# A longer plan for the gated DeltaNet loop, its gates in two buffers, and a new order of transfers around the loop

## The chip, the cores and the metric

The kernel runs on one core of a Trainium2 chip. TensorE (PE) multiplies, VectorE (DVE), ScalarE (ACT) and GpSimd (POOL) do elementwise work, and SyncE (SP) issues the DMA transfers. The metric is the device time of one execution in microseconds, as the median of several runs.

## The reference

A two-layer encoder over one sequence of 1024 tokens, 1024 wide, in float32. Layer 0 mixes tokens by softmax attention, layer 1 by a bidirectional gated DeltaNet; both are followed by a gated MLP with a width-3 convolution.

```python
# attention, 8 heads of 128, 2 kv heads
q, k, v, gate = split(rmsnorm(h) @ w_in)
o = softmax(rope(norm(q)) @ rope(norm(k)).T) @ v * sigmoid(gate);  h += o @ w_out
# gated DeltaNet, 8 q/k heads, 16 v heads of 128, both directions summed
qkv, z, ab = split(rmsnorm(h) @ w_in)          # z: one gate row block for each v head
q, k, v = split(silu(depthwise_conv5(qkv)))
S = S * exp(g) + k.T @ (u - (w @ S));  o = q @ S + attn @ v_new     # chunk by chunk
h += (rmsnorm(o_fwd + o_bwd) * silu(z)) @ w_out
# MLP, 2816 wide, after each mixer
a, b = split(depthwise_conv3(rmsnorm(h) @ w_up));  h += (silu(a) * b) @ w_down
```

## The kernel before

The program has four stages in a row: attention (L230), MLP 0 (`ffn_layer`, L352), gated DeltaNet (`gdn`, L878), MLP 1, and a last norm. Each float32 matrix product is done as three products of a high and a low part (`dense`, L126): `split` (L108) casts a tile to its high part on ACT (L109) and subtracts it on DVE or POOL for the low part (L110), so each block of weights costs a DMA, an ACT cast and a subtraction before PE can use it.

**The DeltaNet loop.** The q, k, v and z products of eight heads, their 5-tap convolutions, the inverses of the chunks' triangular matrices, two chains of eight chunk steps for each head (one in each direction) and the heads' outputs are six flows that a planner, `Weave` (L983), merges into one order for PE. A flow yields pairs: the PE time it has just issued, and an allowance, the plan time that must go by before it is asked again. `mark(name, after)` sets a plan time from which a flow that yielded that name may go on. Flows are asked in the order chains, inverses, prepare, decays, heads_out, products, so the products (L450) fill what the others leave. Only PE's order comes from the plan (`manual_schedule`); the other engines' order comes from a scheduler that goes by priority, and `ahead(n)` (L79) raises the priority of what is issued inside it. Each engine then works through its list in order, whatever the plan's times were.

The places that the change touches: `products` loads and splits the weights, multiplies (PE L490 in `steps`), and either convolves the row (`conv5`: ACT L443, four DVE L446, ACT silu L447) and marks it 20 us later, or, for a z row, takes silu and writes it to DRAM. `prepare` (L494) transposes the rows (PE L576) for k, the grams (PE L547) and the v rows. `heads_out` (L842) squares a half head's output o, multiplies the sums on DVE (L859, twice), raises them to a power (DVE L152, POOL L153, DVE L861), scales o on POOL (L863, eight times), and after an allowance of 16 us transposes it (PE L871), multiplies by the gate tile z (DVE L872) and stores it to DRAM as `od`. z is loaded by DMA at L868 into one buffer; it is overwritten by L872 and stored from there (L873). PSUM holds two `mm` tiles for products, one bank `sp` for all transposes and grams, one bank `ip` for inverses and two `cp` for chains.

**Around the loop.** The first half of the output projection (heads 0 to 3) is the last part of the products flow; the second half (`out_proj`, L326) follows the loop and reads heads 4 to 7 back from `od` through `split_rows` (DMA L941), staged in two slots of `w_raw`. In attention, the first four score blocks (`Heads.first`, L1369; PE L1387, ACT exp L1393) stand together ahead of the eight gate projections (ACT sigmoid L291). The MLP's up-projection (L1021) uses seven half-size products for eight; `operands` forms sums of weight blocks (L1125), and for the first two f takes spare tiles of `gp`. The down-projection (L1187) does the same over 11 blocks p: product 11, 21 (into four `sp` banks), t1 (same banks again), t2, and so on; t1's weights are s = a21 + a22 (DVE L1270), residuals are loaded into `res` tiles.

Of the kernel before, what the change touches and what calls it, by code (L numbers as in the profile page):

```python
# [18 lines left out]
P = 128  # L19
# [22 lines left out]
class Trunk:  # L42
# [187 lines left out]
    def attention(self):  # L230
# [3 lines left out]
        with ExitStack() as ctx, ExitStack() as right:  # L234
# [9 lines left out]
            with tc.tile_pool(reuse_waits="tile", name="yp", bufs=KT) as yp, tc.tile_pool(reuse_waits="tile", name="rp", bufs=1) as rp:  # L244
# [73 lines left out]
                for h in range(1, NH):  # L318
                    gate(h, proj(NH + 2 + h))
            olo = ctx.enter_context(tc.tile_pool(reuse_waits="tile", name="olo", bufs=1))  # L320
            with tc.tile_pool(reuse_waits="tile", name="qp", bufs=2) as qp, tc.tile_pool(reuse_waits="tile", name="pt", bufs=4) as ptp:
# [30 lines left out]
    def ffn_layer(self, layer):  # L352
        tc = self.tc
        xd = self.spill_h(f"xf{layer}_", PARTS)
        with ExitStack() as ctx:
            down = DownProjection(self, layer, xd, ctx)
            with tc.tile_pool(reuse_waits="tile", name="us", bufs=1) as us:
                up = UpProjection(self, layer, us, down.gp)
# [91 lines left out]
    def products(self, ys, tmp, begun):  # L450


        nc, w, cw = self.nc, self.ap["gdn_in"], self.cw5
        rows = [(j, n, i) for j in range(8) for n, i in (("k", 8 + j), ("q", j), ("z0", 32 + 2 * j), ("v0", 16 + 2 * j),
                                                        ("v1", 17 + 2 * j), ("z1", 33 + 2 * j))]
        parts = [(i, k) for _, _, i in rows[2:] for k in (0, 4)]
        split = []

        def fetch():
            if len(split) < len(parts):  # L460
                i, k = parts[len(split)]
                with self.ahead(1):
                    split.append(self.weights(w[i][:, k:k + 4]))

        fetch()
        for p, (j, name, i) in enumerate(rows):
            if p < 2:
                acc = begun[p]
            else:
                acc = self.big()  # L470
                for h in range(2):
                    fetch()
                    for step in self.steps(acc, split[2 * p - 4 + h], ys[4 * h:4 * h + 4], HALVES, h == 0, h == 1):
                        yield step
            if name[0] == "z":
                self.gate_rows(2 * j + int(name[1]), acc, tmp)
            else:
                with self.ahead(2):
                    self.rows[j, name] = self.conv5(acc, cw[:, i], tmp)
                self.weave.mark((name, j), 20.0)  # L480
        for step in self.first_out():
            yield step
# [11 lines left out]
    def prepare(self, tmp, dp):  # L494
# [5 lines left out]
        for j in range(8):  # L500
# [16 lines left out]
            for h, hs in enumerate(HALVES):  # L517
                t = tmp.tile([P, H2], F32, name="h", bufs=2)
                nc.scalar.copy(out=t, in_=self.transposed(kT[:, hs]))
                sums(t, ss[0][:, 4 * h:4 * h + 4])  # L520
                kn.append(t)
                yield 0.44, 1.2
            r = self.rstd(ss[0], 1, dp)
            for h, hs in enumerate(HALVES):
# [4 lines left out]
                put(2, kn[h], slice(4 * h, 4 * h + 4))  # L529
            yield 0.0, 9.0  # L530
            for h, hs in enumerate(HALVES):
# [23 lines left out]
            for h, hs in enumerate(HALVES):  # L555
                sums(self.transposed(qT[:, hs]), ss[1][:, 4 * h:4 * h + 4])
                yield 0.44, 2.8
            r = self.rstd(ss[1], 1, dp)
            self.rq.append(dp.tile([P, NC, 2], F32, name="rq", bufs=2))
            nc.vector.tensor_scalar(out=self.rq[j], in0=r.unsqueeze(2).broadcast_to([P, NC, 2]),  # L560
                                    scalar1=float(P) ** -0.5, scalar2=None, op0=ALU.mult)
            for e in range(2):
                yield f"v{e}", j
                v = self.rows[j, f"v{e}"]
                for h, hs in enumerate(HALVES):
                    t = tmp.tile([P, H2], F32, name="h", bufs=2)
                    nc.scalar.copy(out=t, in_=self.transposed(v[:, hs]))
                    put(3 + e, t, slice(4 * h, 4 * h + 4))
                    yield 0.44, 1.2
            self.weave.mark(("rows", j), 5.0)  # L570
# [271 lines left out]
    def heads_out(self, dp):  # L842
# [3 lines left out]
        for j in range(8):  # L846
            od = [self.dram.tile([P, S], F32, name=f"od{2 * j + e}") for e in range(2)]
            for i in (1, 0):
# [13 lines left out]
                for m in range(8):  # L862
                    nc.gpsimd.tensor_scalar(out=of[:, m], in0=of[:, m], scalar1=rs[:, m:m + 1], scalar2=1.0,  # L863
                                            op0=ALU.mult, op1=ALU.mult)
                yield 0.0, 16.0
                for e in range(2):
                    z = dp.tile([P, H2], F32, name="z", bufs=1)
                    nc.sync.dma_start(out=z, in_=self.zd[2 * j + e][:, hs])  # L868
# [4 lines left out]
                    nc.sync.dma_start(out=od[e][:, hs], in_=z)  # L873
                    yield 0.44, 1.5
            self.od += od
            self.weave.mark(("head", j))

    def gdn(self):  # L878
        nc, tc, ap = self.nc, self.tc, self.ap
        self.pk, self.rq, self.zd, self.od = [], [], {}, []  # L880
        with ExitStack() as left, ExitStack() as right:
# [18 lines left out]
            tc.cur_priority += 1000000  # L900
            oy, st = [], []
            self.outs, self.rows, self.grams, self.decayed, self.solved = {}, {}, {}, {}, {}

            def first_out():
                yps.close()
                oy.append(left.enter_context(tc.tile_pool(reuse_waits="tile", name="oy", bufs=KT)))
                st.append(left.enter_context(tc.tile_pool(reuse_waits="tile", name="st", bufs=1)))
                yield "head", 3
                os = self.split_rows(self.od[:8], oy[0], [slice(0, S)], lambda: tmp.tile([P, S], F32, name="t"))
                yield 0.0, 6.0  # L910
                for m in range(KT):
# [4 lines left out]
                    for i, hs in enumerate(HALVES):  # L916
                        r = st[0].tile([P, H2], F32, name="r")
                        nc.sync.dma_start(out=r, in_=xd[m][:, hs])
# [102 lines left out]
class UpProjection:  # L1021

    def __init__(self, trunk, layer, us, gp):
        self.t, self.nc, self.us, self.gp, self.b = trunk, trunk.nc, us, gp, trunk.b
        self.w = trunk.ap["ffn_up"][layer]
# [100 lines left out]

    def product(self, acc, ops, name, onto=False):

        x, col = ops[name]
        hi, lo = self.t.pair(self.t.wp, "w", H2)
        self.t.split(x, hi, lo, self.nc.gpsimd if name in ("p6", "p4") else self.nc.vector)
        w = [(hi[:, k * P:(k + 1) * P], lo[:, k * P:(k + 1) * P]) for k in range(4)]
        self.t.dense(acc, w, self.b[col], [slice(0, H2)], onto=onto)

    def run(self, up, down):
# [8 lines left out]
        for f in range(NFF):  # L1146
# [13 lines left out]
            with t.ahead(early):  # L1160
# [26 lines left out]
class DownProjection:  # L1187
# [52 lines left out]
    def run(self):  # L1240
# [11 lines left out]

        def product(name, x, accs, ms=range(4), ys=None, onto=False):
# [9 lines left out]

        def residual(m, i):
            r = gm.tile([P, H2], F32, name="res", bufs=3)
            nc.sync.dma_start(out=r, in_=self.xd[m][:, HALVES[i]])
            return r

        def add(out, x, z, engine=nc.vector):
            engine.tensor_tensor(out=out, in0=x, in1=z, op=ALU.add)  # L1270

# [15 lines left out]
        b = [t.bank() for _ in range(4)]  # L1287
        for m, acc in product("11", w1, a, ys=lambda p: self.ready[p] if p < G_FIRST else self.tokens("11", p)):
            add(h(m, 0), acc, residual(m, 0))
# [13 lines left out]
        b = [t.bank() for _ in range(4)]  # L1303
        for m, acc in product("t1", w5, b):
            add(h(4 + m, 1), acc, residual(4 + m, 1))

        def w6(p):
# [3 lines left out]
            return weights(s[p])  # L1311

        for m, acc in product("t2", w6, a, onto=True):
            add(h(m, 1), acc, residual(m, 1))
        for m, acc in product("t3", lambda p: weights(sub(a21[p], a11[p], a21[p])), a, onto=True):
# [8 lines left out]
        for m, acc in product("t4", w4, a, onto=True):  # L1324
            add(h(4 + m, 0), acc, residual(4 + m, 0))
            done(4 + m, 0, False)
# [21 lines left out]
class Heads:  # L1348
# [187 lines left out]
```

## Time and profile before

| | |
|---|---|
| median of 3 runs | 3536.3 us (3531.94 to 3542.98) |
| profiled execution, its own time | 3547.57 us |
| its span | 3545.4 us |
| mean granted TensorE clock | 0.963 |
| PE busy | 3263.7 us (92%) |
| DVE busy | 2478.2 us (70%) |
| ACT busy | 1732.9 us (49%) |
| POOL busy | 922.7 us (26%) |

PE is busy for most of the span, so what matters is where PE stands idle and what it then waits for, and where its granted clock is at the lower of its two levels (1.2 instead of 2.4 GHz, shown as 0.5 of full speed). The loop with its planner runs from 1369.1 to 2734.6 us; attention and MLP 0 come before, the output projection's second half, MLP 1 and the last norm after.

### The profile page before, as it was taken

The numbers are of one execution on the slowest core, as the hardware profiler recorded it, in microseconds if no ns is written. First come the engines' busy times: TensorE is split into PE (matmuls) and PEld (weight loads), VectorE is DVE, ScalarE is ACT, GpSimd is POOL, SyncE is SP. The second block draws the span as 40 slices with busy tenths as digits, with TensorE's granted clock in tenths as the row PEclk, the third lists the DMA queues.
The fourth block names the chain that finished last, engine by engine and source line by source line (L and its number), as shares of the span: only waits on it lengthen the run. The fifth ranks groups of instructions, "written<-read, shape, count | busy, mean of one in ns | idle before, by whom it ended". The sixth has DMA issues, their size and how long they took to land. (4 is left out here: it accounts for less than half of the span.)

```text
span 3545.4 us, 54292 instructions
## 1 busy us (share of the span) xinstructions
PE 3263.7 (92%) x19690; PEld 2649.4 (75%) x19690; DVE 2478.2 (70%) x4199; ACT 1732.9 (49%) x3212; POOL 922.7 (26%) x1111
## 2 busy tenths in 40 slices
PE   7999999799999998897898978989889989999998
PEld 6877878677778786686776866767667867777776
DVE  5325886878776866686776767576754778777685
ACT  4225664445444444455554645556442545454443
POOL 1111220444441001123232313232212154444100
PEclk9999999999999999998999989999899989999999
DMA  3331107333325633233333323333245733322553
GB/s 123 104 108 56 37 28 220 99 110 101 107 87 191 192 121 99 79 103 102 101 116 97 109 88 100 98 99 116 85 153 170 245 107 97 113 95 98 196 164 110
DMA packets 249228, 410.17 MB, mean 116 GB/s; under 512 B 25472, under 2 KB 76032, under 8 KB 248960
## 3 DMA queue, kind: packets, MB, share of 16 engines
q1 hardware_dynamic: 248960, 406.71, 36.5%
q8 instruction: 155, 2.54, 0.3%
q14 instruction: 113, 0.93, 0.1%
HBM read 293.76 MB, written 107.61 MB: 113 GB/s over the span
## 5 line engine op out<-in xcount | busy, mean ns | idle before, releaser
L490 PE MATMUL mm<-base,wh 128*128 128x512 f32 x864 | 389.3, 451 | 15.3 <-DVE t L446 14.8
L110 DVE TENSOR_TENSOR wl<-w_raw,wh 128x512 fp32r<-128x512 f32 x271 | 191.6, 710 | 196.2 <-ACT wh L109 174.6
L109 ACT CAST wh<-w_raw 128x512 fp32r<-128x512 f32 x271 | 167.1, 618 | 305.2 <-PE mm L134 108.4
L153 POOL TENSOR_TENSOR rs<-rs,power 128x8 f32<-128x8 f32 (+2 forms) x38 | 68.0, 1788 | 867.3 <-DVE rs L152 864.8
L109 ACT CAST wh<-s 128x512 fp32r<-128x512 f32 x216 | 134.1, 621 | 230.9 <-PE sp L134 118.0
L109 ACT CAST wh<-a 128x512 fp32r<-128x512 f32 x164 | 101.7, 621 | 261.9 <-PE mm L134 129.7
L134 PE MATMUL sp<-base,wh 128*128 128x512 f32 (+1 forms) x672 | 212.6, 375 | 7.6 <-ACT wh L109 6.7
L797 POOL TENSOR_SCALAR kd<-c,yds 128x128 f32<-128x128 f32 x224 | 96.1, 442 | 473.3 <-PE cp L829 368.1
L490 PEld LDWEIGHTS mm<-base,wh 128*128 128x128 f32 x864 | 168.2, 195 | 40.4 <-issue 15.3
L490 PE MATMUL mm<-base,wl 128*128 128x512 f32 x432 | 193.8, 449 | 0.0
L490 PE MATMUL mm<-yh,wl 128*128 128x512 f32 x432 | 174.4, 404 | 0.0
L446 DVE SCALAR_TENSOR_TENSOR t<-mm,gdn_cw,t 128x1023 f32<-128x1023 f32 (+1 forms) x128 | 163.0, 1276 | 15.0 <-ACT t L443 14.4
L490 PE MATMUL mm<-yl,wh 128*128 128x512 f32 x432 | 173.4, 401 | 0.2
L490 PE MATMUL mm<-yh,wh 128*128 128x512 f32 x432 | 173.4, 401 | 0.0
L110 DVE TENSOR_TENSOR wl<-s,wh 128x512 fp32r<-128x512 f32 x174 | 145.5, 837 | 25.9 <-ACT wh L109 25.5
L134 PE MATMUL sp<-base,wl 128*128 128x512 f32 (+1 forms) x432 | 158.7, 367 | 0.9 <-DVE wl L110 0.9
L134 PEld LDWEIGHTS sp<-base,wh 128*128 128x128 f32 x672 | 128.1, 191 | 30.8 <-ACT wh L109 9.5
L1125 POOL TENSOR_TENSOR s<-a,a 128x512 f32<-128x512 f32 x80 | 105.9, 1323 | 158.8 <-DVE s L1125 99.9
L1203 POOL TENSOR_TENSOR t<-t,t 128x512 f32<-128x512 f32 x66 | 102.6, 1554 | 126.4 <-DVE t L1181 124.6
L1396 POOL TENSOR_SCALAR p<-p,m 128x1024 f32<-128x1024 f32 x60 | 68.3, 1138 | 233.9 <-DVE m L1395 171.3
L110 DVE TENSOR_TENSOR gl<-raw,gh 128x512 fp32r<-128x512 f32 x132 | 97.2, 737 | 31.9 <-ACT gh L109 31.6
L110 POOL TENSOR_TENSOR wl<-s,wh 128x512 fp32r<-128x512 f32 x42 | 75.2, 1790 | 168.3 <-ACT wh L109 168.3
(535 smaller groups left out, 10162.8 us busy)
## 6 DMA issues: line engine op xcount, KB each, us to landing
a<-in_ffn_up_dram SPq DMA_DIRECT2D x160, 256.0 KB, 3.0
c<-pk SPq DMA_DIRECT2D x128, 320.0 KB, 3.0
w_raw<-in_gdn_in_dram SPq DMA_DIRECT2D x100, 256.0 KB, 2.9
g_t<-t SPq DMA_DIRECT2D x88, 256.0 KB, 2.0
raw<-g_t SPq DMA_DIRECT2D x88, 256.0 KB, 2.7
g<-t SPq DMA_DIRECT2D x66, 256.0 KB, 2.1
raw<-g SPq DMA_DIRECT2D x66, 256.0 KB, 3.0
a<-in_ffn_down_dram SPq DMA_DIRECT2D x66, 256.0 KB, 4.4
```

What stands on the lines that cost most here:

```text
L109: self.nc.scalar.copy(out=hi, in_=src)
L110: (engine or self.nc.vector).tensor_tensor(out=lo, in0=src, in1=hi.bitcast(F32), op=ALU.subtract)
L134: self.nc.tensor.matmul(acc if one else acc[:, hs], lhsT=a, rhs=y[:, hs], start=(first and not onto and k + t == 0), stop=(last and k == n ...
L153: nc.gpsimd.tensor_tensor(out=r, in0=v, in1=self.power[:, :w], op=ALU.pow)
L446: nc.vector.scalar_tensor_tensor(out=o, in0=a, scalar=c[:, i:i + 1], in1=o, op0=ALU.mult, op1=ALU.add)
L490: self.nc.tensor.matmul(acc[:, hs] if len(halves) > 1 else acc, lhsT=a, rhs=y[:, hs], start=(first and k + t == 0), stop=(last and k == n ...
L797: nc.gpsimd.tensor_scalar(out=kd[:, e], in0=kn, scalar1=col(self.yds, e), scalar2=1.0, op0=ALU.mult, op1=ALU.mult)
L1125: e.tensor_tensor(out=s[i], in0=x, in1=z, op=op)
L1203: sub = lambda out, x, z: nc.gpsimd.tensor_tensor(out=out, in0=x, in1=z, op=ALU.subtract)
L1396: nc.gpsimd.tensor_scalar(out=p, in0=p, scalar1=m[:, 3:4], scalar2=1.0, op0=ALU.mult, op1=ALU.mult)
```

## The change

The planner's allowances grow: 20 to 24 us behind a convolution, 9 to 15 behind the k norms, 1.2 to 2.0 behind transposes, 16 to 26 and 1.5 to 2.5 in the heads' outputs. The products flow waits for four marks, so that a product of the next head doesn't start before the rows or grams that it would crowd are through. The gate tile z gets two buffers, and its weights' splits higher priority. `r` (the residual of the output projection's first half) moves from a pool of its own to `tmp`'s "h". The reading back of heads 4 to 7 moves into `tmp`'s three "t" slots, ahead of the closing of that pool. In attention, four score blocks move between the gate projections. In the MLP, the first f has two more spare tiles and product p7's split is issued early; in the down-projection product 21's weight pairs come from the weights' pool instead of the tiles of a21 and a22, t1's work from p = 3 on is issued behind the adds that empty product 21's banks, and residuals are loaded straight into the tiles of h.

```diff
@@ attention()
                 for h in range(1, NH):
                     gate(h, proj(NH + 2 + h))
+                    if h < 5:
+                        heads.scores(0, self.base(3 + h, F32))
@@ Heads.first()
         self.queries(0, [self.t.base(k)[:, :H2] for k in (2, 3)])
-        for i in range(4):
-            self.scores(0, self.t.base(4 + i, F32))
@@ ffn_layer(): UpProjection gets down.rp too
@@ products()
-                with self.ahead(1):
+                with self.ahead(3):
                     split.append(self.weights(w[i][:, k:k + 4]))
...
             if p < 2:
                 acc = begun[p]
             else:
+                back = {"k": "queries", "z0": "first rows", "v0": "rows", "z1": "gram"}.get(name)
+                if back and (j or name == "z1"):
+                    yield back, j - (name != "z1")
                 acc = self.big()
...
-                self.weave.mark((name, j), 20.0)
+                self.weave.mark((name, j), 24.0)
@@ prepare()
                 kn.append(t)
-                yield 0.44, 1.2
+                yield 0.44, 2.0
...
-            yield 0.0, 9.0
+            yield 0.0, 15.0
...
+            self.weave.mark(("queries", j))
             r = self.rstd(ss[1], 1, dp)
...
                     put(3 + e, t, slice(4 * h, 4 * h + 4))
-                    yield 0.44, 1.2
+                    yield 0.44, 2.0
+                if e == 0:
+                    self.weave.mark(("first rows", j))
@@ heads_out()
-                yield 0.0, 16.0
+                yield 0.0, 26.0
                 for e in range(2):
-                    z = dp.tile([P, H2], F32, name="z", bufs=1)
+                    z = dp.tile([P, H2], F32, name="z", bufs=2)
...
-                    yield 0.44, 1.5
+                    yield 0.44, 2.5
@@ gdn()
-                        r = st[0].tile([P, H2], F32, name="r")
+                        r = tmp.tile([P, H2], F32, name="h", bufs=2)
...
+            os = self.split_rows(self.od[8:], oy[0], HALVES, lambda: tmp.tile([P, S], F32, name="t")[:, :H2])
             right.close()
-            os = self.split_rows(self.od[8:], oy[0], HALVES, lambda: self.wp.tile([P, H2], F32, name="w_raw", bufs=2))
@@ UpProjection.operands(): spare tiles for the first two f
-            free = iter([self.gp.tile([P, H2], F32, name=n) for n in (3 - f) * ("gh", "gl")])
+            free = [self.gp.tile([P, H2], F32, name=n) for n in (3 - f) * ("gh", "gl")]
+            free = iter(free if f else free + [self.rp.tile([P, H2], F32, name="raw") for _ in range(2)])
@@ UpProjection.product() and run()
+        with self.t.ahead(early):
+            self.t.split(x, hi, lo, self.nc.gpsimd if name in ("p6", "p4") else self.nc.vector)
...
-            self.product(a, ops, "p7", onto=True)
+            self.product(a, ops, "p7", onto=True, early=early)
@@ DownProjection.run()
             for p in range(NP):
-                w = x(p)
-                y = ys(p) if ys else self.tokens(name, p)
+                with t.tc.issue_after(after.ins) if after and p > 2 else nullcontext():
+                    w = x(p)
+                    y = ys(p) if ys else self.tokens(name, p)
...
-            r = gm.tile([P, H2], F32, name="res", bufs=3)
-            nc.sync.dma_start(out=r, in_=self.xd[m][:, HALVES[i]])
-            return r
+        def residuals(ms, i):
+            for m in ms:
+                nc.sync.dma_start(out=h(m, i), in_=self.xd[m][:, HALVES[i]])
...
-        w2 = lambda p: weights(self.load(a12[p], 0, 1, p), [one(n, p, F32R) for n in ("a21", "a22")])
-        for m, acc in product("21", w2, b):
-            add(h(m, 0), acc, h(m, 0))
+        for m, acc in product("21", lambda p: weights(self.load(a12[p], 0, 1, p)), b):
+            read = add(h(m, 0), acc, h(m, 0))
...
-        for m, acc in product("t1", w5, b):
-            add(h(4 + m, 1), acc, residual(4 + m, 1))
+        residuals(range(4, 8), 1)
+        for m, acc in product("t1", w5, b, after=read):
+            add(h(4 + m, 1), acc, h(4 + m, 1))
...
```

**Order of DVE ahead of head 4's output (first half).** `o<-cp,o` is a chain step, `L446`/`L448` a convolution tap, `ss<-ss,rq` (L859, after: L868) the sums from which the output's norm starts; `pr`, `at`, `al` are decays, `wk`, `w_...`, `x` inverses. Before:

```order
L604 TENSOR_TENSOR pr<-pr,qks 128x512
L607 TENSOR_TENSOR al<-at,ah 128x512
L688 STREAM_TRANSPOSE wk<-tp 128x512
L808 SCALAR_TENSOR_TENSOR r_22316<-cp,negc,c 128x128 x2
L814 SCALAR_TENSOR_TENSOR o<-cp,egc,o 128x128 x2
L690 COPY w_11722<-wk 32x16x32 x4
L596 SCALAR_TENSOR_TENSOR pr<-pr,ebias,maskneg 128x128 x4
L446 SCALAR_TENSOR_TENSOR t<-mm,gdn_cw,t 128x1023
L603 TENSOR_TENSOR at<-pr,kks 128x512
L446 SCALAR_TENSOR_TENSOR t<-mm,gdn_cw,t 128x1022
L604 TENSOR_TENSOR pr<-pr,qks 128x512
L859 TENSOR_TENSOR ss<-ss,rq 128x8
```

After:

```order
L697 STREAM_TRANSPOSE wk<-tp 128x512
L704 TENSOR_TENSOR x<-ip,lvl 128x512
L699 COPY w_11706<-wk 32x16x32 x4
L612 TENSOR_TENSOR at<-pr,kks 128x512
L605 SCALAR_TENSOR_TENSOR pr<-pr,ebias,maskneg 128x128
L613 TENSOR_TENSOR pr<-pr,qks 128x512
L605 SCALAR_TENSOR_TENSOR pr<-pr,ebias,maskneg 128x128 x3
L110 TENSOR_TENSOR wl<-w_raw,wh 128x512
L448 SCALAR_TENSOR_TENSOR t<-mm,gdn_cw,t 128x1022 x2
L448 SCALAR_TENSOR_TENSOR t<-mm,gdn_cw,t 128x1023 x4
L448 SCALAR_TENSOR_TENSOR t<-mm,gdn_cw,t 128x1022 x2
L868 TENSOR_TENSOR ss<-ss,rq 128x8 x2
```

Eight taps of two convolutions, in two runs of both kinds, now stand together ahead of the sums, where two taps stood among other work.

**Order of DVE between product 21 and t1 in MLP 0's down-projection.** `s_...<-a_...,a_...` is t1's weight sum (it needs two weight loads), `h_...<-sp` empties a bank of product 21. Before:

```order
L1270 TENSOR_TENSOR s_10051<-a_5_10029,a_5_10040 128x512
L110 TENSOR_TENSOR gl<-raw,gh 128x512
L1270 TENSOR_TENSOR s_10052<-a_6_10030,a_6_10041 128x512
L110 TENSOR_TENSOR gl<-raw,gh 128x512
L1270 TENSOR_TENSOR s_10053<-a_7_10031,a_7_10042 128x512
L1273 TENSOR_TENSOR a_7_10031<-a_7_9651,a_7_10031 128x512
L1270 TENSOR_TENSOR h_9495<-sp,h_9495 128x512
L1270 TENSOR_TENSOR h_9496<-sp,h_9496 128x512
L1270 TENSOR_TENSOR h_9497<-sp,h_9497 128x512
L1270 TENSOR_TENSOR h_9498<-sp,h_9498 128x512
```

After:

```order
L110 TENSOR_TENSOR gl<-raw,gh 128x512
L110 TENSOR_TENSOR wl<-base_9752,wh 128x512
L110 TENSOR_TENSOR gl<-raw,gh 128x512
L110 TENSOR_TENSOR wl<-s_10042,wh 128x512
L110 TENSOR_TENSOR gl<-raw,gh 128x512
L110 TENSOR_TENSOR wl<-s_10043,wh 128x512
L1280 TENSOR_TENSOR h_9495<-sp,h_9495 128x512
L1280 TENSOR_TENSOR h_9496<-sp,h_9496 128x512
L1280 TENSOR_TENSOR h_9497<-sp,h_9497 128x512
L1280 TENSOR_TENSOR h_9498<-sp,h_9498 128x512
```

Before, the four adds stand behind eight of the eleven sums; after, behind three (the first three sums stand further up, at s_10042 to s_10044).

**Order of SP at the end of the loop.** `od` is a head's stored output that is read back, `w_raw<-in_gdn_out_dram` the weights of the output projection's second half. Before:

```order
L121 DMA w_raw<-in_gdn_out_dram 128x512 x2
L941 DMA w_raw<-od_26782 128x512
L918 DMA r<-xd_11476 128x512
L941 DMA w_raw<-od_26783 128x512
L121 DMA w_raw<-in_gdn_out_dram 128x512 x2
L941 DMA w_raw<-od_20773 128x512
L920 DMA x_11874<-r 128x512
L941 DMA w_raw<-od_20774 128x512
L121 DMA w_raw<-in_gdn_out_dram 128x512
L341 DMA res<-x_11867 128x512
```

After:

```order
L882 DMA od_27110<-z 128x512
L949 DMA t<-od_27109 128x512
L949 DMA t<-od_27110 128x512
L949 DMA t<-od_21251 128x512
L949 DMA t<-od_21252 128x512
L949 DMA t<-od_23040 128x512
L949 DMA t<-od_23041 128x512
L949 DMA t<-od_25143 128x512
L949 DMA t<-od_25144 128x512
L949 DMA t<-od_27109 128x512
L949 DMA t<-od_27110 128x512
L121 DMA w_raw<-in_gdn_out_dram 128x512 x5
```

The weights stood among the reads of `od`, two loads after two reads; they now stand behind the reads of all four heads. The first two reads shown need the stores of head 7 just ahead of them, the other eight are the second halves of all rows.

## Rows read from the trace of the kernel before

**Rows 1.** Busy time by stretch: the loop, and two stretches at head 6's output.

```profile
core 0: us, PE busy (x) PEld busy (x) DVE busy (x) ACT busy (x) POOL busy (x), PEclk, DMA share, GB/s
1369.10:2734.60 1365.50, 1206.92 (x10154) 976.15 (x10154) 946.10 (x2115) 713.77 (x1565) 334.06 (x685) 0.94 0.35 107
2532.00:2544.00 12.00, 0.67 (x4) 0.27 (x2) 9.41 (x24) 3.14 (x4) 2.25 (x3) 0.66 0.13 44
2544.00:2556.00 12.00, 9.38 (x94) 6.96 (x94) 4.88 (x15) 4.66 (x18) 2.22 (x7) 0.78 0.22 67
```

**Rows 2.** PE's waits: what it waited for, us in total, times, longest.

```profile
PE sp L871 <- POOL o L863: 49.9, 19, 11.9
PE sp L576 <- DVE z L872: 26.2, 11, 3.8
PE sp L576 <- ACT t L447: 20.5, 3, 7.8
PE sp L134 <- ACT wh L109: 18.6, 4, 7.7
PE sp L134 <- DVE h L1270: 16.5, 2, 10.5
...
PE mm L490 <- DVE t L446: 14.8, 2, 10.7
PE sp L871 <- DVE z L872: 8.0, 2, 6.1
...
PE mm L1387 <- ACT base L1393: 4.7, 1, 4.7
...
PE sp L547 <- DVE z L872: 2.9, 1, 2.9
...
PE mm L1387 <- DVE base L110: 1.6, 1, 1.6
```

**Rows 3.** Timeline at head 6's output: start, duration, engine, line, tile, count, idle before.

```profile
2530.78 0.42 DVE L839 TENSOR_TENSOR o<-cp,o 128x256 f32<-128x256 f32 x1
...
2531.91 0.59 PE L805 MATMUL cp<-st,c 128*128 128x256 f32 x2
...
2536.20 1.28 DVE L446 SCALAR_TENSOR_TENSOR t<-mm,gdn_cw,t 128x1023 f32<-128x1023 f32 x1
...
2539.78 0.16 DVE L859 TENSOR_TENSOR ss<-ss,rq 128x8 f32<-128x8 f32 x1
...
2541.38 1.65 POOL L153 TENSOR_TENSOR ro<-ro,power 128x8 f32<-128x8 f32 x1 [16.60 <-DVE ro L152]
...
2543.40 2.81 POOL L863 TENSOR_SCALAR o<-o,ro 128x128 f32<-128x128 f32 x8 [0.37 <-DVE ro L861]
...
2543.83 0.48 PE L871 MATMUL sp<-ident,o 128*128 128x128 f32 x1 [11.33 <-POOL o L863]
```

**Rows 4.** Timeline at head 0's output, where z's one buffer is stored and loaded.

```profile
1627.25 0.74 DVE L872 SCALAR_TENSOR_TENSOR z<-sp,gdn_gain,z 128x512 f32<-128x512 f32 x1
...
1630.04 0.33 SPq L868 DMA_DIRECT2D z<-zd  x1
...
1633.90 0.74 DVE L872 SCALAR_TENSOR_TENSOR z<-sp,gdn_gain,z 128x512 f32<-128x512 f32 x1
```

**Rows 5.** ACT's timeline at a transposition of k that came late.

```profile
1607.47 1.28 ACT L447 ACT_TABLE_LOAD   x1
1608.77 1.06 ACT L447 ACTIVATE t<-t 128x1024 f32<-128x1024 f32 x1
```

**Rows 6.** Timeline of SP's queue and PE at the end of the loop.

```profile
2736.40 0.33 SPq L941 DMA_DIRECT2D w_raw<-od  x1
...
2738.23 0.32 SPq L941 DMA_DIRECT2D w_raw<-od  x1
...
2739.20 1.22 PE L134 MATMUL sp<-base,wh 128*128 128x512 f32 x2 [4.65 <-ACT wh L109]
...
2760.50 0.80 PE L134 MATMUL sp<-base,wh 128*128 128x512 f32 x2 [2.09 <-ACT wh L109]
```

**Rows 7.** ACT's timeline at the first scores, and two gate projections later on.

```profile
209.27 1.28 ACT L1393 ACT_TABLE_LOAD   x1 [6.55 <-DVE m L1391]
210.56 1.21 ACT L1393 ACTIVATE base<-mm,m,scale 128x1024 f32<-128x1024 f32 x1
...
240.35 1.02 ACT L291 ACTIVATE t<-mm 128x1024 f32<-128x1024 f32 x1
...
251.23 1.02 ACT L291 ACTIVATE t<-mm 128x1024 f32<-128x1024 f32 x1
```

**Rows 8.** DVE's timeline between product 21 and t1.

```profile
1159.25 0.69 DVE L1270 TENSOR_TENSOR s<-a,a 128x512 f32<-128x512 f32 x1 [1.70 <-DMA a<-in_ffn_down_dram]
...
1160.58 2.48 DVE L1270 TENSOR_TENSOR h<-sp,h 128x512 f32<-128x512 f32 x4
```

More of the change, by code (lines that the diff above doesn't have):

```diff
@@ L1 @@
-from contextlib import ExitStack, contextmanager
+from contextlib import ExitStack, contextmanager, nullcontext
 from functools import partial
@@ L357, in ffn_layer @@
             with tc.tile_pool(reuse_waits="tile", name="us", bufs=1) as us:
-                up = UpProjection(self, layer, us, down.gp)
+                up = UpProjection(self, layer, us, down.gp, down.rp)
                 up.tokens(self.gain_ffn[:, layer])
@@ L900, in gdn @@
             tc.cur_priority += 1000000
-            oy, st = [], []
+            oy = []
             self.outs, self.rows, self.grams, self.decayed, self.solved = {}, {}, {}, {}, {}
@@ L906, in first_out @@
                 oy.append(left.enter_context(tc.tile_pool(reuse_waits="tile", name="oy", bufs=KT)))
-                st.append(left.enter_context(tc.tile_pool(reuse_waits="tile", name="st", bufs=1)))
                 yield "head", 3
@@ L1021, with __init__ @@
 class UpProjection:
-    def __init__(self, trunk, layer, us, gp):
-        self.t, self.nc, self.us, self.gp, self.b = trunk, trunk.nc, us, gp, trunk.b
+    def __init__(self, trunk, layer, us, gp, rp):
+        self.t, self.nc, self.us, self.gp, self.rp, self.b = trunk, trunk.nc, us, gp, rp, trunk.b
         self.w = trunk.ap["ffn_up"][layer]
@@ L1127, in operands, with product @@
                 "p4": (a22, "t4"), "p3": (s[3], "22")}
-    def product(self, acc, ops, name, onto=False):
+    def product(self, acc, ops, name, onto=False, early=0):
         x, col = ops[name]
         hi, lo = self.t.pair(self.t.wp, "w", H2)
-        self.t.split(x, hi, lo, self.nc.gpsimd if name in ("p6", "p4") else self.nc.vector)
+        with self.t.ahead(early):
+            self.t.split(x, hi, lo, self.nc.gpsimd if name in ("p6", "p4") else self.nc.vector)
         w = [(hi[:, k * P:(k + 1) * P], lo[:, k * P:(k + 1) * P]) for k in range(4)]
@@ L1251, in weights, with product @@
             return pair
-        def product(name, x, accs, ms=range(4), ys=None, onto=False):
+        def product(name, x, accs, ms=range(4), ys=None, onto=False, after=None):
             for p in range(NP):
-                w = x(p)
-                y = ys(p) if ys else self.tokens(name, p)
+                with t.tc.issue_after(after.ins) if after and p > 2 else nullcontext():
+                    w = x(p)
+                    y = ys(p) if ys else self.tokens(name, p)
                 for m in ms:
@@ L1262, in product @@
             return [(m, accs[m]) for m in ms]
-        def residual(m, i):
-            r = gm.tile([P, H2], F32, name="res", bufs=3)
-            nc.sync.dma_start(out=r, in_=self.xd[m][:, HALVES[i]])
-            return r
+        def residuals(ms, i):
+            for m in ms:
+                nc.sync.dma_start(out=h(m, i), in_=self.xd[m][:, HALVES[i]])
         def add(out, x, z, engine=nc.vector):
-            engine.tensor_tensor(out=out, in0=x, in1=z, op=ALU.add)
+            return engine.tensor_tensor(out=out, in0=x, in1=z, op=ALU.add)
         def sub(out, x, z, engine=nc.vector):
@@ L1287, in run @@
         b = [t.bank() for _ in range(4)]
-        for m, acc in product("11", w1, a, ys=lambda p: self.ready[p] if p < G_FIRST else self.tokens("11", p)):
-            add(h(m, 0), acc, residual(m, 0))
+        acc11 = product("11", w1, a, ys=lambda p: self.ready[p] if p < G_FIRST else self.tokens("11", p))
+        residuals(range(4), 0)
+        for m, acc in acc11:
+            add(h(m, 0), acc, h(m, 0))
         a12 = [x[:, hs] for x in [t.base(i, F32) for i in range(2, 8)] for hs in HALVES][:NP]
-        w2 = lambda p: weights(self.load(a12[p], 0, 1, p), [one(n, p, F32R) for n in ("a21", "a22")])
-        for m, acc in product("21", w2, b):
-            add(h(m, 0), acc, h(m, 0))
+        for m, acc in product("21", lambda p: weights(self.load(a12[p], 0, 1, p)), b):
+            read = add(h(m, 0), acc, h(m, 0))
             done(m, 0, m == 0)
@@ L1311, in w6 @@
             return weights(s[p])
+        residuals(range(4), 1)
         for m, acc in product("t2", w6, a, onto=True):
-            add(h(m, 1), acc, residual(m, 1))
+            add(h(m, 1), acc, h(m, 1))
+        residuals(range(4, 8), 0)
         for m, acc in product("t3", lambda p: weights(sub(a21[p], a11[p], a21[p])), a, onto=True):
@@ L1324, in run @@
         for m, acc in product("t4", w4, a, onto=True):
-            add(h(4 + m, 0), acc, residual(4 + m, 0))
+            add(h(4 + m, 0), acc, h(4 + m, 0))
             done(4 + m, 0, False)
```

## The prediction

> **What bounds the kernel now.** I read the busy shares first (PE 92% of the span, DVE 70%), then PE's waits, then the timeline around the longest ones, and last the granted clock by stretch. PE is the bound: what can be won is its idle time, and the time that it works at the lower clock.
>
> In the loop PE is busy 1206.92 of 1365.50 us [rows 1], so 158.6 us are idle. The waits [rows 2] name three groups there. A: PE's transposition of a head's output waits for POOL's scaling, 49.9 us, of which four waits of 11 to 12 us are 46.5 and the rest crumbs. B: a transposition or gram waits for DVE's multiplication by z, 26.2 + 8.0 + 2.9 = 37.1. C: the transposition of k waits for the convolution's silu, 20.5 in three. Together 104.1. A further 14.8 is a product that waits at the start for convolutions to empty a PSUM tile.
>
> How A comes about [rows 3]: PE issues its last possible chain work at 2531.91 and then stands before L871. DVE took up the chain's step at 2530.78, at PE's pace, but has 9.0 us of other work in its list before the sums at 2539.78: taps of 1.28 us, decays, inverse copies. From there sums, power (1.65 on POOL) and first scaling take 4.05 us to L871 at 2543.83. Hence a rule: wait = W + 4.05 - Q, with W the DVE work between a chain step and the sums in DVE's list, and Q the PE work between the same step and L871 in PE's list. With the profile's durations the old lists give 11 to 12 for heads 3 to 6, and four waits of that size are there. The plan's allowance (16 us) doesn't see W.
>
> B [rows 4]: the one z tile is read by L872 at 1627.25, stored, loaded again from 1630.04, and used at 1633.90: 6.65 us in which the sp bank stays full. C [rows 5]: four taps wait in DVE's list, a table load of 1.28 us comes, silu takes 1.06.
>
> The clock in the loop is 0.94 of full speed [rows 1]: 0.06 x 1365.5 = 82 us of full-speed time is missing. Part of it falls into the waits themselves: at head 6 the 12 us with the wait ran at 0.66 (4.1 lost, mostly idle), the next 12 at 0.78 (2.6 lost, working). By that ratio 32 us would be lost to work, and 82 is the upper end.
>
> **The loop, term by term.** B: with two z tiles, both loads go out ahead of the head's output, and the sp bank is emptied 0.75 us after its transposition: -37. C: the mark moves from 20 to 24 us and the transpositions' allowances from 1.2 to 2.0; I take it all, -20.5. A: the allowance of 26 gives Q some 4 to 10 us more, but DVE's list changes too. In the order ahead of head 4, W is one stream transpose, one x, four copies, at, pr, wl (each about 0.6 net), four decays (1.1) and eight taps at 1.19 (9.5): 14.8, and Q counted from PE's order is 5.7: 14.8 + 4.05 - 5.7 = 13.2. Head 2 is alike (W 15.9, Q 5.8: 14.2), head 3 gives 5.4 + 4.05 - 7.1 = 2.4, heads 5 and 6 about nothing (W 8.1 and 10.1 against Q 11.9 and 12.2), but there the last product of a head waits for the tap that empties its PSUM tile, by the same count 6.6 and 6.5. Sum 43, with crumbs of 3 as now 46. So A, B and C together go from 104 to 46: **-58**. From the other side: if a plan with more room removed them all, -104; if the new lists gave nothing back, 0.
>
> Clock: the waits fall by 56%, so by the two ends above 18 to 46 us come back; the new waits are long ones, at whose end the clock is down, so I take **-20**. Start: the product z1 of head 0 now stands behind the first grams, so the wait of 10.7 [rows 2] shrinks, but six steps on the single sp bank have no product beside them, about 1.1 each (a transposition and its 0.6 copy): **-4**. A fuller loop meets DVE (946 us busy, 69% of it, 73% of a loop of 1290) more often; the idle time outside the named waits is 158.6 - 104.1 - 14.8 = 40, and I add an eighth, **+5**.
>
> End of the loop. Now the first L134 waits 4.65 and another 2.09 [rows 6]; the reads of `od` alternate with weight loads through two slots, 1.83 us apart. After the change the head's last transpositions stand directly before L134, where products stood between; the weights are queued on SP behind all reads, and the eight second-half reads go through three slots. Store about 2 (od at 1628.01 to the next load at 1630.04, the pair around [rows 4]), eight reads at 1.4 to 1.75 (two slots give about 2.6 a read over the stretch, three two thirds of it), then load 2.9 and cast 0.6: 2 + 13 + 3.5, about 20 instead of 6.7: **+13**. If the queue runs ahead, 0; if stores and reads don't overlap at all, +28. Loop and end: -64.
>
> **The other stages.** Attention: the waits 4.7 and 1.6 [rows 2] come from the scores standing together; spread between projections 10.9 us apart [rows 7], each block has a projection to hide reduction and exp. With 2.6 for the clock after it (the stretch after head 6's wait) that is -8.9. Exp and sigmoid alternate, six more table loads of 1.28 [rows 7]. An exp's load starts only when DVE is done (209.27, after 6.55 idle), but it lies under the next projection; a sigmoid's load carries no wait for PE and can go early, so I charge 1: **-8**. If the sigmoid's load lay on PE's path it would be 4 x 1.28 = 5.1 more, so -3; the chance of that is 0.2.
>
> The Trainium skill (ScalarE: Activation LUTs, "What ACT_TABLE_LOAD costs") speaks against the alternation: each change of set costs 2.66 us, 1283 ns of load and the rest a drain. The trace agrees on the load (1.28) and shows exp at 210.56 right after it, so no drain behind the load; were the full price on PE's path, the four would cost 10.6 and attention would be slower by 2.6.
>
> MLP up, both layers: the casts of p7 and t3 make 18.6 - 6.7 = 11.9 us of L134's waits. Two more spare tiles let the sums go without waiting for tiles, and the early split puts p7's cast ahead of later work; DVE remains busy there, so I take two thirds, -8, and 3 for the clock: **-11** (-2 to -16).
>
> MLP down, both layers: 16.5 [rows 2]. The four adds that empty product 21's banks took 2.48 us, but began only when eight sums had passed, each waiting for a weight load (1.70 before the last) [rows 8]. In the new order they stand behind three sums, whose loads no longer wait for product 21's pairs. What is left is the first add's 0.6 and a semaphore, 1.5 each: -13.5, and 2.6 of clock each: **-19**. What is late next is t1's own weights; there the residual loads, issued earlier on SP, could stand before them, at 0.4 us each: up to +3. Range -5 to -21.
>
> Sum: -64 - 8 - 11 - 19 = **-102**. The profiled execution took 3547.57, so 3445.6 for its like; it lies 11.3 above the median of the runs, and from the median 3536.3 the sum gives **3434 us**.
>
> **Rivals.**
> 1. DVE becomes the bound of the loop. For: its lists decide A and C, and allowances only move waits. Against: 946 us in 1365 leaves 420 idle. Then A stays at 46 with the taps' waits on top: 104 falls to about 90, clock gives 5, and the sum is -14 - 5 - 4 + 5 + 13 - 38 = -43: 3493.
> 2. The change doesn't do what it says at z: the second tile's load stands behind a store or a `pk` transfer on SP, so B stays (37 us, with 8 of clock): 3434 + 45 = 3479. For: SP is one list, and 37 us came through it. Against: the order has z's loads in pairs ahead of the transpositions.
> 3. Slower: the taps gather before the sums at every half head. Place: DVE's list between the chain step and L868. Eight taps instead of two to three add about 7 us to W; where Q doesn't grow, waits of 11.6 become 19, and over the seven heads 1 to 7 that is 133 instead of 104, clock +15. It decides once DVE's lag at a head passes the 26 us of allowance less 4. Sum: +29 + 15 + 13 - 38 + 5 = +24: 3560. For: heads 2 and 4 show it. Against: heads 3, 5, 6 don't.
>
> **How the numbers follow.** My forecast 0.60, alone with a range of 3395 to 3475 (from the loop's waits between 20 and 75 and its end between 0 and +28). Rival 1 0.20, rival 2 0.11, rival 3 0.09. To leave out no more than a fifth the range runs from 3395 to 3525. A measurement tells 0.3% (10.6 us) from no change, so faster means under 3525.7: all of my forecast and rival 2, most of rival 1: 0.86. Slower 0.08, none to be told 0.06.
>
> **What would show it.** In the new profile B's waits on z are gone, A's rows show two waits of 13 to 14 (heads 2 and 4) and none at 5 and 6, products waiting for taps appear with about 6 us, the first L134 after the loop waits near 20, the loop is near 1290 us. In the MLPs the wait on `h` falls to about 3 in total. Wrong: a loop above 1330 us, more than two waits over 10 us on POOL, or exp's table loads ending PE's waits.

## The result, and the profile after

The change made the kernel faster, by much less than forecast: 3517.78 us (median of 4) against 3538.47, ratio 0.9941 [0.9923, 0.9959], so -20.7 us where -102 were expected. The two profiled executions lie 33 us apart (spans 3545.4 and 3512.4), since that of before took longer than any of the four timed runs (3547.6 against at most 3543.0) and that of after is the fastest of its four; the sums by stage below go by these two, and so overstate the gain by 12 us in all.

| stretch | forecast | before | after | difference |
|---|---|---|---|---|
| up to the loop's first product | -23 | 1369.1 | 1354.3 | -14.8 |
| the loop | -77 | 1365.5 | 1348.8 | -16.7 |
| wait behind the loop | +13 | 4.65 | 20.14 | +15.5 |
| from there to the end | -15 | 806.2 | 789.2 | -17.0 |

Most of what is missing lies in the loop. Outside it these two executions look near the forecast, but the 12 us must be taken off somewhere, and x1 below measures less. Busy time of the loop after (columns as in [rows 1]):

```profile
1354.30:2703.10 1348.80, 1210.31 (x10154) 987.26 (x10154) 943.73 (x2116) 701.23 (x1556) 333.87 (x685) 0.94 0.37 109
```

The clock is 0.94 as before, the idle time 138 instead of 159. PE's waits in the loop after, which answer to [rows 2]:

```profile
PE mm L496 <- DVE t L448: 45.7, 5, 13.9
PE ip L669 <- DVE w L683: 18.1, 10, 11.2
PE sp L880 <- POOL o L872: 10.8, 16, 2.2
PE sp L880 <- DVE z L881: 9.5, 4, 4.5
PE sp L585 <- ACT t L449: 6.7, 2, 3.8
PE ip L764 <- ACT r L760: 6.3, 10, 2.0
PE sp L553 <- DVE kks L555: 5.7, 4, 3.3
PE cp L832 <- DVE r L817: 5.4, 5, 4.2
PE cp L813 <- issue: 4.8, 2, 2.7
```

The groups A (49.9 to 10.8), B (37.1 to 9.5 and crumbs) and C (20.5 to 6.7) have indeed shrunk to a quarter. In their place products wait for convolution taps (four of 7 to 14 us in the loop, and 5.0 ahead of its first product), and inverses, grams and chains wait for DVE. DVE's and PE's timelines at the longest wait:

```profile
1883.81 9.60 DVE L448 SCALAR_TENSOR_TENSOR t<-mm,gdn_cw,t 128x1022 f32<-128x1022 f32 x8
1893.33 0.35 DVE L868 TENSOR_TENSOR ss<-ss,rq 128x8 f32<-128x8 f32 x2
```

```profile
1892.28 0.79 PE L496 MATMUL mm<-base,wh 128*128 128x512 f32 x1 [13.87 <-DVE t L448]
...
1896.41 0.47 PE L880 MATMUL sp<-ident,o 128*128 128x128 f32 x1 [1.42 <-POOL o L872]
```

These are eight taps in a row ahead of head 2's sums, as DVE's order showed for head 4; they make the product z1 wait first, and the output after it. SP's queue at the loop's end, and PE behind it, answer to [rows 6]:

```profile
2703.92 0.32 SPq L882 DMA_DIRECT2D od<-z  x1
2704.51 12.58 SPq L949 DMA_DIRECT2D t<-od  x10
2719.86 3.24 SPq L121 DMA_DIRECT2D w_raw<-in_gdn_out_dram  x5
```

```profile
2723.24 1.22 PE L134 MATMUL sp<-base,wh 128*128 128x512 f32 x2 [20.14 <-ACT wh L109]
```

The ten reads take 12.6 us, and the first weights are issued only after them.

### The profile page after: what moved, and what is told of

It is laid out like the page before. It is cut to its first block, busy times and chain, and to the rows that moved or that the text cites. A ratio compares the mean times of both kernels' runs of the same rounds, so it can differ in the third digit from the quotient of the medians.

```text
span 3512.4 us, 54302 instructions
## 1 busy us (share of the span) xinstructions
PE 3250.7 (93%) x19690; PEld 2645.6 (75%) x19690; DVE 2471.1 (70%) x4199; ACT 1725.4 (49%) x3209; POOL 920.3 (26%) x1111
## 5 line engine op out<-in xcount | busy, mean ns | idle before, releaser
L448 DVE SCALAR_TENSOR_TENSOR t<-mm,gdn_cw,t 128x1023 f32<-128x1023 f32 (+1 forms) x128 | 161.7, 1275 | 7.0 <-ACT t L445 6.1
L109 ACT CAST gh<-raw 128x512 fp32r<-128x512 f32 x132 | 81.7, 619 | 117.6 <-DMA raw<-g_t 67.2
```

The costliest lines, as they stand in the source:

```text
L109: self.nc.scalar.copy(out=hi, in_=src)
L448: nc.vector.scalar_tensor_tensor(out=o, in0=a, scalar=c[:, i:i + 1], in1=o, op0=ALU.mult, op1=ALU.add)
```

## The experiments

Two kernels serve as bases: the changed kernel, and the **short plan**: attention and MLPs as changed, all of the loop's plan and the reading back as before, z in two tiles and r in `tmp`'s "h". Each median is of 4 or 5 executions; "before" was 3538 to 3540 us beside each. "Waits" is the sum of PE's idle times of 1 us and more in the loop, "low" the time in it at 0.5 of full clock, both summed from the trace.

| run | median us | ratio to before | loop | waits | low |
|---|---|---|---|---|---|
| before | 3538.5 | | 1365 | 131 | 153 |
| changed kernel | 3517.8 | 0.9941 [0.9923, 0.9959] | 1349 | 109 | 154 |
| x1: loop as before, z one tile | 3524.3 | 0.9962 [0.9949, 0.9974] | 1363 | 128 | 160 |
| x2: short plan | 3484.8 | 0.9855 [0.9842, 0.9869] | 1322 | 104 | 117 |
| x3: changed, old reading back | 3508.1 | 0.9920 [0.9906, 0.9933] | 1345 | 108 | 143 |
| x4: changed, taps first | 3558.9 | 1.0060 [1.0046, 1.0073] | 1382 | 119 | 159 |
| x5: x2 + holds | 3518.2 | 0.9942 [0.9929, 0.9956] | 1354 | 116 | 163 |
| x6: x3, short head allowance | 3526.5 | 0.9964 [0.9952, 0.9977] | 1365 | 121 | 157 |
| x7: x2 + early fetch | 3498.2 | 0.9877 [0.9861, 0.9893] | 1335 | 118 | 131 |
| x8: x2, outputs 3 | 3477.0 | 0.9824 [0.9810, 0.9837] | 1314 | 90 | 112 |
| x9: x2, outputs 6 | 3494.7 | 0.9875 [0.9860, 0.9890] | 1336 | 118 | 121 |
| x10: x9, decays 1 | 3447.0 | 0.9736 [0.9721, 0.9750] | 1284 | 63 | 60 |
| x11: x10, taps 4 | 3504.0 | 0.9897 [0.9880, 0.9913] | 1340 | 101 | 108 |
| x12: x3, outputs 6, decays 1 | 3478.2 | 0.9827 [0.9813, 0.9841] | 1310 | 92 | 62 |

**x1**, the loop's part undone (all allowances, holds, fetch, z, r and reading back as before).

> The loop, its allowances, its one z tile, the pool of r and the reading back of heads 4 to 7 are as before; attention and both MLPs are as in the changed kernel. Theory 1 (the gain lies outside the loop; inside, waits only moved): the stretches outside the loop were 14.8 us and, without the wait at the loop's end, 30.4 us shorter in the changed kernel's trace, so about -32 us against before (ratio 0.991), the loop at 1365 us with its three groups of waits, the wait behind the loop 5 to 7 us. The forecast's reading (-64 in loop and end, -38 outside) would give -38. Rival (the loop gained and a later stage lost it): below 10 us.

-13.8 against before (-9 to -18 by the interval): less than half of what either theory expected of the outside, and above the rival's 10. The loop is 1363 us with the old waits. In the profiled execution, 22 us shorter than that of before, 12 of the gain lie ahead of the loop and 7 behind it.

**x2**, as x1 with

```diff
-z = dp.tile([P, H2], F32, name="z", bufs=1)
+z = dp.tile([P, H2], F32, name="z", bufs=2)
-r = st[0].tile([P, H2], F32, name="r")
+r = tmp.tile([P, H2], F32, name="h", bufs=2)
```

> The same with z in two tiles (and r in tmp's h, since its own pool then doesn't fit). The forecast's step (both gate loads go ahead, the wait on z falls away and nothing takes its place): 37 us of waits on DVE z and some clock go, about -40 against the kernel with z in one tile. Theory 1 (PE meets DVE a little later at the next result it needs): the waits on z fall under 10 us, but waits of other names grow by 20 or more, so -10 to -18.

-39.5 against x1: the forecast's step, and theory 1 falls. The waits on z fell from 34.5 in x1 to 9.0 and little took their place; all idle time of the loop fell by 26 us, PE's busy time by 15, and low by 43 us. The move of r was not tried alone; PE's order is the same in both. This kernel alone beats the changed one by 33 us. PE's waits and the loop's busy time:

```profile
PE sp L880 <- POOL o L872: 50.9, 21, 11.9
PE sp L585 <- ACT t L449: 20.5, 3, 7.7
...
PE sp L880 <- DVE z L881: 8.0, 2, 6.1
...
PE sp L553 <- DVE z L881: 0.6, 1, 0.6
...
PE sp L585 <- DVE z L881: 0.4, 1, 0.4
```

```profile
1358.80:2680.30 1321.50, 1192.06 (x10154) 964.29 (x10154) 945.81 (x2116) 711.63 (x1566) 331.28 (x685) 0.96 0.37 112
```

**x3**, the changed kernel with

```diff
-os = self.split_rows(..., lambda: tmp.tile([P, S], F32, name="t")[:, :H2])
 right.close()
+os = self.split_rows(..., lambda: self.wp.tile([P, H2], F32, name="w_raw", bufs=2))
```

> The changed kernel with heads 4 to 7 read back as before (two w_raw slots, after the pool has closed). The first product behind the loop waited 20.1 us in the changed kernel and 4.7 and 2.1 in the kernel before. Forecast and theory 1 agree: that wait falls to 5 to 8 us, -13 us against the changed kernel, so about -34 against before. Rival (the wait is the last head's own chain, stores and loads, whatever the slots): no change, 18 to 20 us.

-9.7 where -13 was expected, and the wait falls to 7.4 as forecast. Against x1 it is 16 us faster, so part of x1's rival holds: the loop gained and the stage behind it lost. Against x2, which differs only in the plan (allowances, holds, fetch), it is 23 us slower. So the plan, to which some -27 of the forecast's -77 belonged (A and C -21, start -4, +5, and a share of the clock), lost 23.

**x4**, taps above all else: `self.ahead(2)` of `conv5` to `self.ahead(6)`.

> The changed kernel with the convolutions issued at a priority above the chains (ahead 6 instead of 2), nothing else. Theory 1 (what is left in the loop are waits for DVE's list, above all where eight taps gather): products waiting for taps fall from 46 us to under 20, by counting DVE and PE work between chain steps in the new order two waits of 12 and 7 are left; -20 to -35 us against the changed kernel with the clock. Rival (the loop's waits stay at 110 to 130 us whatever the order, since DVE's lag shows up at the next thing that PE needs): the taps' waits are replaced by waits of chains and inverses on DVE, within 10 us of the changed kernel.

41 us slower than the changed kernel, where theory 1 had it 20 to 35 faster. The products' waits for taps fell to 4.1, but inverses waited 39.6 us for DVE, outputs 36.5 for POOL, chains 18.5 for DVE. The rival named what happens (the waits reappear at inverses and chains) and not its size, which it put within 10 us. Counting W and Q only where a wait is known doesn't see it.

**x5**, the short plan with the four holds (`if back and (j or name == "z1"): yield back, ...`).

> The kernel with z in two tiles (3484.8 us: loop allowances as before, reading back as before) plus the four marks that hold products back, no longer allowance. Theory 2 (each part of the longer plan moves PE's waits for DVE from one name to another and none removes them; the holds do it by leaving PE without products to fill): counting DVE's and PE's lists, the waits at the heads' outputs stay near 50, C may go; small waits of inverses and chains grow; within -10 and +15 us of 3484.8. Rival (the holds alone are what costs the changed kernel 23 us): 3505 or more.

33 us slower than x2, the rival's outcome: waits grew by 12, low by 46. In places the holds leave PE few products beside the small steps. At the loop's start, 1395 to 1415 us, the changed kernel, x5 and then x2:

```profile
1395.00:1415.00 20.00, 15.90 (x60) 13.34 (x61) 9.61 (x16) 5.89 (x16) 0.75 (x3) 0.57 0.22 66
```

```profile
1395.00:1415.00 20.00, 14.94 (x64) 12.10 (x63) 9.64 (x12) 8.21 (x16) 4.18 (x9) 0.69 0.27 79
```

```profile
1395.00:1415.00 20.00, 18.52 (x102) 15.17 (x100) 11.95 (x19) 10.40 (x21) 3.00 (x9) 1.00 0.29 90
```

The same 20 us hold 60 or 64 multiplications at a clock of 0.57 or 0.69, or 102 at full clock; all three hold the 32 of the grams, and 16, 20 or 58 of products. This place alone doesn't make x5 slower, though. The next 20 us, x5 and then x2, which now stands at the wait of 10.7:

```profile
1415.00:1435.00 20.00, 19.72 (x136) 15.69 (x135) 19.09 (x34) 10.56 (x26) 3.06 (x3) 0.97 0.43 138
```

```profile
1415.00:1435.00 20.00, 10.75 (x48) 8.88 (x49) 15.80 (x26) 7.39 (x18) 2.07 (x1) 0.74 0.25 77
```

An estimate that gives each multiplication its spacing at full clock in x10's loop has the two level 80 us into the loop (65 us of work each), x5 behind by 10 us at 200 and by 18 at 1200. So the loss is spread over the loop, and that thin stretches make it is argued, not shown.

**x6**, x3 with the outputs' allowances back at 16 and 1.5; **x7**, x2 with `ahead(3)` in `fetch`.

> The changed kernel with the reading back as before and the head outputs' allowances as before (16 and 1.5); its comparison is the same kernel with 26 and 2.5 (3508.1 us). Theory 2: by the lists the waits at the heads' outputs are back (9, 11, 11, 12, 12 us) and products still wait for taps, 3 to 6 us each: 3500 to 3530, no better than with the long allowance. Rival (the 26 us send PE past the point where it should turn to the output, and cost the 23 us): 3480 to 3490.

> The kernel with z in two tiles (3484.8 us) with only the products' weights fetched and split at higher priority (ahead 3 instead of 1). Theory 2: PE's order is the same, the lists of ACT and DVE change a little, waits at the heads' outputs 9 to 12 us as before: within 6 us of 3484.8. Rival (the splits, 1.2 us of DVE each, push taps and decays late and cost the 23 us): 3500 or more.

x6 is 18 us slower than x3, as theory 2 had it: the outputs' allowances of 26 and 2.5 are the part of the plan that pays, once the holds are there. x7 costs 13 us, more than theory 2's 6 and short of its rival: PE's order is that of x2, and inverses (L756) wait 12.0 us for DVE. The parts nearly add up: holds +33, fetch +13, the outputs' allowances -18 make +28, and all is +23; the other allowances have the rest. The long allowances weren't tried without the holds, so it stays open what they give alone.

**x8 to x11**, PE's order as in x2, other engines' lists by priority:

```diff
-(self.decays(dp), 3), (self.heads_out(dp), 1)
+(self.decays(dp), 3), (self.heads_out(dp), 3)   # x8
+(self.decays(dp), 3), (self.heads_out(dp), 6)   # x9
+(self.decays(dp), 1), (self.heads_out(dp), 6)   # x10; x11: also ahead(4) for conv5
```

> The kernel with z in two tiles (3484.8 us), PE's order untouched, but the heads' outputs issued at the priority of prepare and decays (3 instead of 1), so that their sums, powers and scalings stand ahead of decays and taps in the lists of DVE, ACT and POOL. By counting W and Q no wait over 1 us is left at the heads' outputs. Theory 2b (PE's order was good, DVE's list was wrong): four waits of 11 to 12 us go and little comes back, 3484.8 - 30 to - 50. Theory 2 (waits move): taps and decays that are pushed back make products and inverses wait, 3475 to 3490.

> As the kernel with the heads' outputs at the priority of decays (3477.0 us; its four waits at the outputs were still 7.7 to 9.1 us, since taps and decays stood between the sums and the power), but with the outputs' priority above everything (6). Theory 2b: sums, power and products follow each other in DVE's list, the waits at the outputs fall to about 4 us (DVE's lag of some 4 us plus nothing), 3477 - 12 to - 25. Theory 2 (the rest comes back elsewhere): 3470 to 3485.

> The same with the decays' work, the largest part of what stands in DVE's list ahead of outputs and taps, at priority 1 instead of 3 (below the taps' 2). Theory 2b: the transposition of k, which waits 20 us for taps and silu in three waits, gains 5 to 15 us, and the total falls by that: 3445 to 3465. Theory 2: decays come late for the next head's grams and inverses, which then wait; 3470 to 3490.

> The same with the taps at 4 instead of 2, level with the inverses and below the chains. In the changed kernel taps above the chains (6) cost 41 us. Theory 2b (it was the chains that suffered there): the waits for taps (k's transposition, the first products) go down further, 0 to -10 us against the run with late decays. Theory 2: inverses wait for taps as they did there, 5 to 25 us slower than that run.

x8: -8, theory 2's outcome; the four waits fell from 11.3-11.9 to 7.7-9.1. x9: 18 us slower than x8, where both theories had it level or faster; the outputs' waits are gone and k's transposition waits instead:

```profile
PE sp L585 <- ACT t L449: 64.9, 7, 11.7
```

x10: -48 against x9, inside theory 2b's 3445 to 3465. Behind the taps the decays hold up little: the waits for taps fall and no others grow long. Late decays with the outputs at their old priority weren't tried. The first waits of its list, and the loop:

```profile
PE ip L669 <- DVE w L683: 16.5, 13, 4.7
...
PE ip L764 <- ACT r L760: 12.7, 14, 2.5
PE mm L496 <- DVE wl L110: 12.7, 6, 4.6
...
PE sp L585 <- ACT t L449: 2.6, 2, 1.3
```

```profile
1354.40:2638.30 1283.90, 1186.08 (x10154) 959.30 (x10154) 947.33 (x2116) 701.82 (x1562) 332.38 (x685) 0.98 0.38 115
```

No wait of the loop is above 4.7 us, and the clock is 0.98. DVE does the same work (947 us; 944 in the changed kernel's loop, 946 in x2's). x11: taps level with the inverses cost 57 us again (inverses wait 38.1 us for DVE L704): theory 2's direction, more than twice its size.

**x12**, the changed plan on x10's priorities, with the old reading back.

> The changed kernel with the reading back as before (3508.1 us) and with the two priorities of the best run (outputs 6, decays 1): the longer plan on a mended list of DVE. Comparison: the short plan on the same list, 3447.0. Theory 2 (the long plan has no merit of its own: its holds thin PE out, and its allowances cover a lag that the mended list doesn't have): better than 3508 by 20 to 50, but 10 to 30 slower than 3447. Rival (the plan was right and only DVE's list spoilt it): 3447 or less.

30 us better than x3, 31 worse than x10: theory 2, the plan has no merit of its own. Its loop has x10's low time (62 and 60 us), so here the plan costs waits (92 against 63). With the list mended the changed plan leaves these:

```profile
PE ip L669 <- DVE w L683: 37.7, 16, 12.7
...
PE cp L813 <- DVE st L842: 13.0, 13, 3.7
PE cp L832 <- DVE r L817: 10.2, 9, 2.1
```

**The best version** is x10: 3447.0 us, 2.6% below before, from the outside's edits, z's second tile and two priorities.

## Why the prediction was wrong

The direction held; the size didn't. The stated range, 3395 to 3525, holds 3517.8 only because it was drawn out for the rivals; the forecast's own, 3395 to 3475, misses it by 43 us, and one sign of being wrong came, a loop above 1330 us. By medians the miss divides so: the loop -16 (x3 against x1) where -77 was forecast, the outside -14 (x1) where -38 was, the end +10 (x3) where +13 was.

The step that failed first is **"A, B and C together go from 104 to 46: -58"**, read as a fall of PE's idle time. The waits did go, but the loop's idle time fell by 20 us only (158.6 to 138.5): A -39, B -26, C -14, products waiting for taps +30, all other idle time +29. With it failed the clock's -20: PE's busy time rose by 3.

- **B (z's second tile): right in total.** -37 and its part of the clock were forecast; x2 against x1 shows -39.5. The division is partly luck: the waits gave 26 and PE's busy time 15, the clock's part being larger than I put it.
- **A: about right in size.** The forecast had 46 us of waits left from A and from products waiting for taps. There are 51.5 (40.7 for taps in the loop, 10.8 at POOL). They stand elsewhere than I wrote: A's rows show none above 2.2, and the taps' four are 13.9 (head 2), 13.0 (head 4), 6.8 and 7.0 (heads 5 and 6) where 14.2, 13.2, 6.6 and 6.5 were computed. The first two were computed for the output, where z1 met the taps first, so that the agreement to 0.3 us is partly luck: at head 2 PE stood 13.9 and 1.4, 15.3 in all, before the output.
- **C, "I take it all": failed.** C fell from 20.5 to 6.7, but I worked out no W and Q for what PE does next. New waits came at inverses (+11 at L669), grams (5.7) and chains (10 in two rows), more than C gave. All idle time of the loop outside A, B, C and the taps' waits grew from 40 to 69 us, so the "+5" for a fuller DVE was +29.
- **Clock -20: failed.** The low time is 154 us as before. x2 had it down to 117; holds and allowances brought it back (x5 163, x3 143). I tied the clock to the sum of the waits. In x3's loop the low time comes in 20 pieces, in x2's in 13: beside waits of 11 to 14 us, pieces of 3 to 7 us stand at waits of 2 to 7, and one of 17 us, at the loop's start, at no wait above 1.
- **Start -4: about nothing.** The wait of 10.7 went, but a stretch at a clock of 0.57 came; by the estimate used for x5, the changed kernel and the one before had both done 63 us of work 80 us into the loop.
- **End +13: right**, for the reason given. The table's +15.5 counts the first wait alone; with the second, 4.65 + 2.09 became 20.14, +13.4. x3 takes 10 of it back.
- **Outside -38: too much.** It is -14 by x1's median, whose loop is as before's, and -32 in the two profiles. In these attention is 7.7 us shorter (-8 was forecast) and the MLPs together 19.3 (-30); in x1's profile 4.1 and 13.6. In attention the sigmoids' loads end at the sigmoid's start and cost three waits of 2.7 us in all, nearer to the forecast's 1 than to 6.1. In the up-projections the casts' 11.9 are gone, but 6.5 of waits for the low part of a split on DVE came in two places. In the down-projections the first adds wait 1.5 and 1.9 us as computed, but later products wait 3.2 and 1.6 us for the same kind of add.

Of the rivals, the first had the mechanism (DVE's list decides, allowances move waits) and priced the result at 3493; it was nearest, though DVE is not the bound: x10 has it busy for the same 947 us in a loop 82 us shorter than before.

The Trainium skill (TensorE: Matmul & The Clock Gate, Terms) puts the loss to the gate at the low time times a half. The runs agree roughly if only the low time in which PE was busy is counted: from the kernel before to x10 it fell from 90 to 47 us in the loop, which makes 22, and PE's busy time fell by 21. The rest of the low time, 63 and 13 us, lay in idle time. For x5 against x2 the same count makes 24, and PE's busy time is 17 us longer.

## What to carry to other kernels

Where one engine's order is planned and the others' comes from priorities, ask of a wait which work stands ahead of the awaited instruction in the other engine's list, and who needs that work soon: here two priorities in DVE's list gave 38 us (x10 against x2) with PE's order untouched. Raising one kind of work far above the others cost more elsewhere than it gave (x4, x9, x11). A longer allowance mostly moved the meeting point, so compute W - Q for the next two or three meetings as well, before booking a wait as won. And test each part of a composite change alone: here a second tile (with r's move) was worth 40 us and the rest of the plan cost 23.

## What was not expected of the hardware

ACT's timeline of the changed kernel between a sigmoid and an exp:

```profile
225.51 1.02 ACT L291 ACTIVATE t<-mm 128x1024 f32<-128x1024 f32 x1
226.89 1.28 ACT L1405 ACT_TABLE_LOAD   x1 [0.36 <-DVE m L1403]
228.19 1.21 ACT L1405 ACTIVATE base<-mm,m,scale 128x1024 f32<-128x1024 f32 x1
```

The load took 1.28 us and exp began 1.66 us after the sigmoid's end (226.53), 0.36 of it a wait for DVE, so no further drain of a microsecond stands between two tables here. And the clock can be low without any long wait: in the changed kernel's 20 us shown with x5, PE was busy 15.9 of 20 us at a granted clock of 0.57, and no wait in the low stretch of 17 us, or in the 10 us ahead of it, was above 1 us.
